# A hybrid attention layer on one Trainium2 core: where the low-rank stage takes its pages, which engine splits the weights, and how long the program's order waits behind tables and rows

## The chip, the cores and the metric

One core of a Trainium2 chip runs the whole layer. The metric is device time in microseconds of one execution. "Before" and "after" are two kernels that compute the same; the profile is one execution recorded by the hardware profiler. The engines are TensorE (PE, its weight loads PEld), VectorE (DVE), ScalarE (ACT), GpSimd (POOL) and SyncE (SP, which here only issues DMAs, in order).

## The reference

2048 tokens of width 1024 pass one layer. `h = rms_norm(x)`, one projection `h @ w_in`, and three groups of heads share its columns:

```python
c_q, c_kv, k_rope, gdn_qkv, gdn_a, gdn_b, mem_q, gate = split_cols(h @ w_in[l], IN_SPLITS)
q  = (rms_norm(c_q, q_a_norm[l]) @ w_q_b[l])       # low rank 384, then 4 heads, rotary part
kv = (rms_norm(c_kv, kv_a_norm[l]) @ w_kv_b[l])    # low rank 256
o_mla = causal_mla(...)
o_gdn = rms_norm(gated_delta_rule_chunked(...), gdn_norm[l])   # per chunk: T = (I + L)^-1, then a scan
o_mem = memory_attention(...)
x = x + (concat([o_mla, o_gdn, o_mem]) * silu(gate)) @ w_out[l]
return rms_norm(x, norm_final)
```

## The kernel before

All products that need fp32 accuracy are made of three passes: both operands are split into a high part (rounded to the fast format fp32r) and a low part (the rest), and `mm3` adds hi x hi, hi x lo and lo x hi. For the weights the split is `w_split` (L613): `copy` makes `wh` on ScalarE or VectorE, `lesser` (L628) chooses GpSimd or VectorE for `wl = w - wh`. A weight tile `wr` has two buffers, so the load of the tile after next, issued by SyncE, waits until `wl` has read its buffer.

The tokens are worked in two halves of 1024. In each half, 34 column tiles of `w_in` are streamed through TensorE (`ip`), and generators that were spawned by earlier tiles put their work between the products:

- `delta_head` (L843), four per half: norms (`sq`), decay rows (`gr`, loaded back from DRAM) and row factors (`fr`), the products `kk`, then a triangular solve of 31 steps on GpSimd (`pr`, `X`, fed and emptied by GpSimd's own DMAs), the block inverse (`inv`, `mid`), and a scan over 8 chunks. A chunk is a chain: `pa<-k,state` (TensorE), `r` (VectorE), `pa<-r,inv`, `vn` (ScalarE), `pa<-vn,kt`, the new state (VectorE), and beside it two products for the output. Only one scan runs at a time.
- `low_rank` (L1119), two per half ("the key rank" with 2 tiles, products `kb`, `vb`; "the query rank" with 3 tiles, `qb`): for each of two blocks of 512 tokens it loads the raw projection `craw`, squares and sums it, turns it (`sq`), makes the inverse root, spreads it (`rb`) and splits the scaled tiles (`chl`); then it streams small weights (`bw`) through `mm3`. It needs 2n pages of a pool of 10, of which each delta head also holds two or three. The last query tiles get their rotary part from tables (`cs`, `sn`) loaded by `trig_load` (L1183).

Behind the projections come causal attention (`sc`, `pt`, `av`), memory attention and the output projection (`op`).

Nothing of this order is decided on the chip. While the program is built, a planner runs beside it: `note`, `pool_cost`, `pool_dma` and `issue` keep a planned time for each engine, each generator is resumed when TensorE's planned time reaches the time that it yielded (`yield 2000` means 2 us behind the step's planned end), and the instructions are written in that order. Each engine then works its own list strictly in order, so the plan's numbers set which instruction stands in front of which.

Of the kernel before, what the change touches and what calls it, by code (L numbers as in the profile page):

```python
# [15 lines left out]
ALU = mybir.AluOpType  # L16
# [9 lines left out]
NH = 4  # L26
# [16 lines left out]
SPARE = 700.0  # L43
# [7 lines left out]
SLACK = {"wl": 500.0, "bwl": 0.0}  # L51
# [16 lines left out]
def hybrid_layer(ctx, tc, a, out):  # L68
    nc = tc.nc
    V, A, G, PE = nc.vector, nc.scalar, nc.gpsimd, nc.tensor  # L70
# [76 lines left out]
    T = {"PE": 0.0, "DVE": 0.0, "ACT": 0.0, "POOL": 0.0, "SP": 0.0, "DMA": 0.0}  # L147
# [5 lines left out]
    in_psum = set()  # L153
    tiles = set()
    step_end = [0.0]
    solving = [0.0]
    tab = [None]

    def free(ap):
        return int(np.prod(ap.shape[1:]))  # L160
# [61 lines left out]

    def pool_cost(op, args, kw, out):
        if op == "tensor_tensor":
            return 147 + 2.1 * free(out)
        fast = op == "tensor_scalar" and kw["op0"] == ALU.mult and kw.get("op1") == ALU.add
        return 160 + (0.85 if fast or op == "memset" else 3.4) * free(out)

# [18 lines left out]
    class Timed:  # L247
# [3 lines left out]
        def __getattr__(self, op):  # L251
            f = getattr(self.eng, op)

            def call(*args, **kw):
# [6 lines left out]

    V, A, G, PE = (Timed(nc.vector, "DVE", dve_cost), Timed(nc.scalar, "ACT", act_cost),
                   Timed(nc.gpsimd, "POOL", pool_cost), Timed(nc.tensor, "PE", pe_cost))


# [18 lines left out]
    def pool_dma(out, in_):  # L284

        touch(in_, out)
        t = max(T["POOL"], T["PE"], arrival(in_, "POOL"), used.get(out.tensor.name, 0.0),
                floor.get(out.tensor.name, 0.0)) + 600
        T["POOL"] = t
        t += 1500 + free(out) * out.shape[0] * 4 / 200  # L290
        wrote(out, "SP", t + 1000)
        step_end[0] = max(step_end[0], t + 1000)
        used[in_.tensor.name] = max(used.get(in_.tensor.name, 0.0), t + 200)
        pinned(nc.gpsimd.dma_start(out=raw(out), in_=raw(in_)))  # L294
# [32 lines left out]
    POLL = 800.0  # L327
# [22 lines left out]
    done = {}  # L350
# [9 lines left out]
    def take(**need):  # L360
        while not can(**need):
            yield POLL
        grab(**need)
# [250 lines left out]
    def w_split(w):  # L614
        wh = sb.tile([P, 512], F32R, name="wh", tag="wh", bufs=3)
        copy(wh, w)
        wl = sb.tile([P, 512], F32R, name="wl", tag="wl", bufs=3)
        lesser("wl").tensor_tensor(wl, w, wh, op=ALU.subtract)
        return wh, wl

    def copy(out, in_):
# [5 lines left out]

    def lesser(name):  # L628

        return G if max(T["POOL"], solving[0]) <= T["PE"] + SLACK[name] else V  # L630

    class Job:

# [207 lines left out]
        return consume  # L841

    def delta_head(hf, h, q, k, res):  # L843

        yield from take(N=1)
        sums, norms = (sb.tile([P, 16], F32, name=n, tag=n, bufs=b) for n, b in (("sums", 1), ("norms", 4)))
# [49 lines left out]
        for b in range(2):  # L896
            bs = slice(b * 512, (b + 1) * 512)
            nq, nb, ne = (t.rearrange("p (c t) -> p c t", t=P) for t in cur)

            gc = cols[:, 0, h * 8 + b * 4:h * 8 + b * 4 + 4]  # L900
            gr3 = gr.rearrange("p (c t) -> p c t", t=P)
            V.tensor_tensor(gr3, gr3, gc.unsqueeze(2).broadcast_to([P, 4, P]), op=ALU.subtract)
            V.tensor_tensor(gr3, gr3, neg.unsqueeze(1).broadcast_to([P, 4, P]), op=ALU.add)
            A.activation(gr, gr, AF.Exp)
            k3, q3 = (t[:, bs].rearrange("p (c t) -> p c t", t=P) for t in (k, q))
            V.tensor_tensor(kq[:, :, 0, :], k3, nb, op=ALU.mult)
            yield 0
            V.tensor_tensor(kq[:, :, 1, :], q3, nq, op=ALU.mult)
            V.tensor_tensor(q3, q3, ne, op=ALU.mult)
            V.tensor_tensor(gr3, gr3, nk[:, b * 4:b * 4 + 4].unsqueeze(2).broadcast_to([P, 4, P]), op=ALU.mult)  # L910
            yield 0
            if b == 0:
                cur = rows(1)
                yield SPARE
            for c2 in range(2):
                ps = psg("kk")
                for c in range(2):
                    cc = c2 * 2 + c
                    PE.matmul(ps[:, c * 256:(c + 1) * 256], k[:, b * 512 + cc * P:b * 512 + (cc + 1) * P],
                              kq[:, cc, :, :], start=True, stop=True)  # L920
                o = b * 4 + c2 * 2
                ps4 = ps.rearrange("p (c i t) -> p c i t", c=2, i=2)
                dec = gr3[:, c2 * 2:c2 * 2 + 2, :]
                V.tensor_tensor(LT[:, o:o + 2, :], ps4[:, :, 0, :], dec, op=ALU.mult)
                atm = sb.tile([P, 2, P], F32, name="atm", tag="atm", bufs=2)
                V.tensor_tensor(atm, ps4[:, :, 1, :], dec, op=ALU.mult)
                dma(out=at_d[hf][h][:, o * P:(o + 2) * P], in_=atm.rearrange("p c t -> p (c t)"), awaited=False)
                if b == 0 and c2 == 1:
                    gr = decay_row(1)
                yield 0  # L930
        give(A=1)
        done["rows"] = done.get("rows", 0) + 1
        for bk in range(4):
# [8 lines left out]
        pool_dma(out=X, in_=a["eye4"])  # L942
        for cs in range(4):
            pool_dma(out=lt[cs * 32:(cs + 1) * 32].rearrange("p j i -> p (j i)"), in_=lsys[hf][h])
        solving[0] = T["POOL"] + 25000
        yield 2000
        pr = sb.tile([P, 80], F32, name="pr", tag="pr", bufs=1)
        for j in range(31):
            n = j // 4 + 1
            w = 31 - j  # L950
# [3 lines left out]
            G.tensor_tensor(X[:, 0:n, j + 1:32], X[:, 0:n, j + 1:32], prv, op=ALU.subtract)  # L954
        for cs in range(4):
            pool_dma(out=tsys[hf][h].rearrange("s (n e) i -> e s n i", e=4)[cs], in_=X[cs * 32:(cs + 1) * 32])
        solving[0] = T["POOL"] + 12000
        yield from take(TT=1)
        yield 0
        give(lt=1)  # L960
# [8 lines left out]
        for n in (32, 64):  # L969
            pairs = [(2 * n * p, slice(2 * n * p, 2 * n * p + n), slice(2 * n * p + n, 2 * n * p + 2 * n))  # L970
                     for p in range(64 // n)]
            mid = t2("mid", (P, 8 * n))
            mid3 = mid.rearrange("p (c t) -> p c t", t=n)

            def sl(c):
                return slice(c * n, (c + 1) * n)
            for o, lo, hi in pairs:
                for i in range(n // 32):
                    for j in range(i, n // 32):
                        src, dst = slice(o + i * 32, o + i * 32 + 32), slice(o + j * 32, o + j * 32 + 32)  # L980
                        V.transpose(mid3[dst, :, i * 32:i * 32 + 32], TT[src, :, dst])
                        if i < j:
                            G.memset(mid3[src, :, j * 32:j * 32 + 32], 0.0)
            yield 0
            ps = psg("inv")
            for c in range(NCK):
                for o, lo, hi in pairs:
                    PE.matmul(ps[hi, sl(c)], LT[lo, c, hi], mid[lo, sl(c)], start=True, stop=True)
            for o, lo, hi in pairs:
                if o:  # L990
                    A.activation(mid[hi, :], ps[hi, 0:8 * n], AF.Copy, scale=-1.0)
                else:
                    V.tensor_scalar(mid[hi, :], ps[hi, 0:8 * n], -1.0, None, op0=ALU.mult)
            yield 0
            ps = psg("inv")
            for c in range(NCK):
                for o, lo, hi in pairs:
                    PE.matmul(ps[lo, sl(c)], mid[hi, sl(c)], TT[hi, c, hi], start=True, stop=True)
            for o, lo, hi in pairs:
                (A.copy if o else V.tensor_copy)(TT[lo, :, hi], ps[lo, 0:8 * n].rearrange("p (c t) -> p c t", t=n))  # L1000
            yield 0
# [15 lines left out]
        for c in range(NCK):  # L1017
# [32 lines left out]
            t = step_end[0]  # L1050
# [40 lines left out]
    def small_weights(srcs):  # L1091

        def load(src):
            w = sb.tile([P, src.shape[1]], F32, name="bw", tag="m2", bufs=9)
            dma(out=w, in_=src, awaited=False)
            return w

        def split(w):
            n = w.shape[1]
            wh = sb.tile([P, n], F32R, name="bwh", tag="m2", bufs=9)  # L1100
            copy(wh, w)
            wl = sb.tile([P, n], F32R, name="bwl", tag="m2", bufs=9)
            lesser("bwl").tensor_tensor(wl, w, wh, op=ALU.subtract)
            return wh, wl
        w = load(srcs[0])
        yield 2800
        cur = split(w)
        w = load(srcs[1])
        yield 0
        for i in range(len(srcs)):  # L1110
            nxt = None
            if i + 1 < len(srcs):
                nxt = split(w)
                if i + 2 < len(srcs):
                    w = load(srcs[i + 2])
            yield cur
            cur = nxt

    def low_rank(hf, n, gain, srcs, use):  # L1119

        yield from take(page=2 * n)
        hs, ls = ([[], []] for _ in range(2))
        for b in range(2):
# [20 lines left out]
        t = 0  # L1144
# [12 lines left out]
    def q_use():  # L1157
# [9 lines left out]
        def use(hf, t, hs, ls, wh, wl):  # L1167
# [10 lines left out]
            for b in range(2):  # L1178
# [1 line left out]
                cs, sn = t2("cs"), t2("sn")  # L1180
                trig_load(cs, 0, hf * 2 + b, 4)
                trig_load(sn, 1, hf * 2 + b, 4)
                yield 2000  # L1183
                r1, r2 = project(b, hs, ls, *half), project(b, hs, ls, wh, wl)
                tA, tB, tC = t2("ra"), t2("rb"), t2("rc")
                V.tensor_tensor(tA, r1, cs, op=ALU.mult)
# [1010 lines left out]
```

## Time and profile before

| | us |
|---|---|
| median of 3 runs | 1818.56 (1814.57 to 1819.68) |
| the profiled execution's own time | 1822.34 |
| its span, first to last instruction | 1820.6 |
| TensorE busy | 1746.9 (96%) |
| VectorE busy | 1158.6 (64%) |
| ScalarE busy | 734.6 (40%) |
| GpSimd busy | 500.4 (27%) |
| mean granted clock of TensorE | 0.983 |

A matmul counts as busy until its modelled end, and matmuls overlap; what TensorE loses shows as idle time before an instruction and as stretches with a granted clock below 1.0 (at 0.5 it runs at 1.2 instead of 2.4 GHz). An engine that is not TensorE matters where TensorE waits for it, or where it holds a DMA that someone else needs.

### The profile page before, as it was taken

How to read it: one execution, taken by the hardware profiler on the slowest of the kernel's cores; microseconds unless marked ns; L12 is line 12 of the kernel's file. 1: busy time of each engine (PE TensorE's matmuls, PEld its weight loads, DVE VectorE, ACT ScalarE, POOL GpSimd, SP SyncE). 2: the span in 40 equal slices, each digit the busy share in tenths (PEclk: the TensorE clock that was granted, in tenths of full speed). 3: DMA queues.
4: the chain of work that ended last, by engine and by line, in shares of the span. 5: the costliest groups of instructions: out<-in, count | busy, mean ns of one | idle time of the engine just before them, and what ended most of it. 6: DMA issues, size and time to landing. Idle time of an engine off the chain costs nothing.

```text
span 1820.6 us, 28632 instructions
## 1 busy us (share of the span) xinstructions
PE 1746.9 (96%) x9776; PEld 1471.2 (81%) x9776; DVE 1158.6 (64%) x2622; ACT 734.6 (40%) x1884; POOL 500.4 (27%) x894
## 2 busy tenths in 40 slices
PE   7999999999999999899999997999999999999998
PEld 5778788888777777788888876899999998888886
DVE  6777766786785858445566653777676778345443
ACT  6444233342442535213453423455455556222121
POOL 1422752443521124352112625001111012412120
PEclk9999999999999999999999998999999999999999
DMA  7544474456555344564555479145252527566551
GB/s 265 163 128 150 137 237 137 131 160 211 154 170 176 121 147 116 184 194 138 182 199 176 141 216 265 61 127 178 70 177 71 159 88 224 167 195 199 168 162 53
DMA packets 225826, 291.19 MB, mean 160 GB/s; under 512 B 30320, under 2 KB 130672, under 8 KB 225680
## 3 DMA queue, kind: packets, MB, share of 16 engines
q1 hardware_dynamic: 218640, 273.62, 48.3%
q0 software_dynamic: 7040, 15.74, 3.0%
q8 instruction: 77, 1.26, 0.3%
q14 instruction: 69, 0.57, 0.1%
HBM read 197.79 MB, written 91.49 MB: 159 GB/s over the span
## 4 chain that ended last, share of the span: by engine, by line
PE 54%; DMA 4%; DVE 3%; POOL 1%; issue 1%; ACT 1%; SPq 1%; DVEq 0%; ACTq 0%; POOLq 0%
PE op L259 14%; PE ip L259 13%; PE sc L259 9%; PE av L259 7%; PE pt L259 4%; PE pa L259 2%; PE qb L259 1%; PE inv L259 1%; DVE y L259 1%; PE kk L259 1%; DMA craw<-craw 1%; SPq L305 1%; PE kb L259 1%; PE mk L259 1%; POOL X L259 1%
## 5 line engine op out<-in xcount | busy, mean ns | idle before, releaser
L259 PE MATMUL ip<-hh,wh 128*128 128x512 f32 x1088 | 459.8, 423 | 12.6 <-ACT hh L259 9.1
L259 PE MATMUL ip<-hh,wl 128*128 128x512 f32 x1088 | 433.8, 399 | 5.1 <-DVE wl L259 4.0
L259 PE MATMUL ip<-hl,wh 128*128 128x512 f32 x1088 | 432.3, 397 | 0.0
L259 POOL TENSOR_TENSOR wl<-wr,wh 128x512 fp32r<-128x512 f32 x84 | 120.2, 1431 | 493.9 <-ACT wh L259 403.9
L259 PEld LDWEIGHTS ip<-hh,wl 128*128 128x128 f32 x1088 | 208.3, 191 | 52.7 <-DVE wl L259 4.5
L259 PEld LDWEIGHTS ip<-hh,wh 128*128 128x128 f32 x1088 | 209.1, 192 | 49.5 <-ACT hh L259 9.1
L259 PEld LDWEIGHTS ip<-hl,wh 128*128 128x128 f32 x1088 | 209.2, 192 | 35.4 <-DVE hl L259 0.5
L259 ACT CAST wh<-wr 128x512 fp32r<-128x512 f32 x144 | 88.9, 618 | 148.6 <-PE ip L259 99.1
L259 DVE TENSOR_TENSOR tl<-pt,th 128x512 fp32r<-128x512 f32 (+2 forms) x208 | 119.8, 585 | 32.6 <-ACT th L259 30.2
L259 PE MATMUL av<-th,vn 128*128 128x256 f32 x576 | 133.2, 290 | 1.9 <-ACT th L259 1.9
L259 PE MATMUL sc<-kn,qn 128*128 128x512 f32 (+2 forms) x480 | 134.0, 379 | 0.0
L259 PE MATMUL op<-wop,mh 128*128 128x512 f32 x416 | 130.6, 394 | 0.0
L259 DVE SCALAR_TENSOR_TENSOR y<-raw,gdn_conv,y 128x512 f32<-128x512 f32 x144 | 116.5, 814 | 16.1 <-ACT y L259 14.7
L259 ACT CAST th<-pt 128x512 fp32r<-128x512 f32 (+2 forms) x160 | 80.6, 512 | 105.6 <-PE pt L259 98.7
L259 POOL TENSOR_TENSOR pr<-X,lt 128x60 f32<-128x60 f32 (+24 forms) x248 | 92.4, 373 | 49.2 <-DMA lt<-lsys 30.3
L259 PEld LDWEIGHTS av<-th,vn 128*128 128x128 f32 x576 | 99.2, 189 | 6.8 <-ACT th L259 3.0
L259 POOL TENSOR_TENSOR X<-X,pr 128x60 f32<-128x60 f32 (+24 forms) x248 | 95.9, 386 | 19.4
L294 POOL DMA_DIRECT2D mix<-mo x64 | 34.8, 544 | 226.5 <-ACT mo L259 186.8
L259 PE MATMUL sc<-kr,qr 128*128 128x512 f32 (+2 forms) x320 | 96.7, 380 | 0.0
L259 ACT ACTIVATE s<-s,m 128x768 f32<-128x768 f32 (+13 forms) x71 | 79.0, 1114 | 41.7 <-DVE mx L259 35.2
L259 PEld LDWEIGHTS op<-wop,mh 128*128 128x128 f32 x416 | 77.4, 188 | 17.5
L259 PE MATMUL pt<-ident,s 128*128 128x128 f32 x544 | 84.2, 276 | 6.2 <-DVE vt L259 6.0
(285 smaller groups left out, 3522.5 us busy)
## 6 DMA issues: line engine op xcount, KB each, us to landing
wr<-in_w_in SPq DMA_DIRECT2D x148, 256.0 KB
fr<-rows_n SPq DMA_DIRECT2D x48, 256.0 KB
mxo<-mix SPq DMA_DIRECT2D x16, 768.0 KB
craw<-craw SPq DMA_DIRECT2D x40, 256.0 KB
x<-in_xT SPq DMA_DIRECT2D x32, 256.0 KB
gatem<-gt SPq DMA_DIRECT2D x32, 256.0 KB
qn<-qn SPq DMA_DIRECT2D x32, 256.0 KB
vn<-v SPq DMA_DIRECT2D x32, 256.0 KB
```

The costliest lines, as they stand in the source:

```text
L259: return pinned(f(*args, **kw))
L294: pinned(nc.gpsimd.dma_start(out=raw(out), in_=raw(in_)))
L305: ins = pinned(nc.sync.dma_start(out=raw(out), in_=raw(in_)))
```

## The change

- In the second half (`hf` = 1) `low_rank` asks for pages only when the fourth delta head has started (`done[("head", hf, h)]`, set by `delta_head` at its start).
- `w_split` and the small weights make their low part on VectorE always. `lesser` stays for the opening tiles alone; the guard `solving`, which kept splits off GpSimd during a planned solve, is gone.
- The plan's costs of GpSimd's elementwise work and of its DMAs are larger.
- The generators yield longer at four places: 2500 behind the issue of the second decay row, SPARE (700) twice per level of the inverse, 5000 instead of 2000 behind the rotary tables.

```diff
-    solving = [0.0]
...
         if op == "tensor_tensor":
-            return 147 + 2.1 * free(out)
+            return 290 + 2.25 * free(out)
...
-        t += 1500 + free(out) * out.shape[0] * 4 / 200
+        t += 2500 + free(out) * out.shape[0] * 4 / 200
...
         wl = sb.tile([P, 512], F32R, name="wl", tag="wl", bufs=3)
-        lesser("wl").tensor_tensor(wl, w, wh, op=ALU.subtract)
+        V.tensor_tensor(wl, w, wh, op=ALU.subtract)
...
-        return G if max(T["POOL"], solving[0]) <= T["PE"] + SLACK[name] else V
+        return G if T["POOL"] <= T["PE"] + SLACK[name] else V
...
     def delta_head(hf, h, q, k, res):
 
+        done[("head", hf, h)] = True
...
                 if b == 0 and c2 == 1:
                     gr = decay_row(1)
-                yield 0
+                    yield 2500
+                else:
+                    yield 0
...
-        solving[0] = T["POOL"] + 25000
...
-        solving[0] = T["POOL"] + 12000
...
-            yield 0
+            yield SPARE
             ps = psg("inv")
...
-            yield 0
+            yield SPARE
             ps = psg("inv")
...
-            lesser("bwl").tensor_tensor(wl, w, wh, op=ALU.subtract)
+            V.tensor_tensor(wl, w, wh, op=ALU.subtract)
...
     def low_rank(hf, n, gain, srcs, use):
 
+        while hf and not done.get(("head", hf, NH - 1)):
+            yield POLL
         yield from take(page=2 * n)
...
                 trig_load(sn, 1, hf * 2 + b, 4)
-                yield 2000
+                yield 5000
```

The plan's numbers move instructions on every engine: 95 splits from GpSimd to VectorE, and the order of most rows from the first weight product on. Three places show it.

GpSimd, second half, between the solves of the first and second head (`X`, `lt`, `pr` belong to the solve, `tsys` and `inv` carry its result to DRAM and back, `wl` is a weight split that reads the load buffer `wr`). Before:

```order
L259 TENSOR_TENSOR X_7109<-X_7109,pr_7223 128x8
L294 DMA tsys1_0_109<-X_7109 256x1x32 x4
L294 DMA inv0_279<-tsys1_0_109 32x8x32 x4
L294 DMA X_7847<-in_eye4 128x256
L259 TENSOR_TENSOR wl_7655<-wr_7553,wh_7653 128x512
L259 MEMSET mid_7770 32x8x32
L294 DMA lt_7846<-lsys1_1_102 32x1024 x4
L259 TENSOR_TENSOR pr_7934<-X_7847,lt_7846 128x31
```

In the change:

```order
L258 TENSOR_TENSOR X_7584<-X_7584,pr_7689 128x8
L293 DMA tsys1_0_109<-X_7584 256x1x32 x4
L293 DMA inv0_279<-tsys1_0_109 32x8x32 x4
L293 DMA X_8522<-in_eye4 128x256
L258 MEMSET mid_8365 32x8x32
L293 DMA lt_8521<-lsys1_1_102 32x1024 x4
L258 TENSOR_TENSOR pr_8635<-X_8522,lt_8521 128x31
```

The split of `wr_7553` stood behind eight DMAs of the solve; in the change GpSimd's list there holds the solve alone.

SyncE, second half, around the load of the second decay row `gr` (`at` stores a product of the same head, `bw` and `wr` are weight loads, `qn` stores of the query rank, `mk` stores and loads of the memory projection). Before:

```order
L305 DMA bw_7779<-in_w_q_b 128x384
L305 DMA at1_1_78<-atm_7575 128x256
L305 DMA wr_7857<-in_w_in 128x512
L305 DMA qn1_2_143<-ehi_7597 128x512
L305 DMA gr_7608<-rows_g_62 128x512
L305 DMA qn1_2_143<-elo_7598 128x512
L305 DMA at1_1_78<-atm_7606 128x256
```

In the change:

```order
L304 DMA wr_8374<-in_w_in 128x512
L304 DMA mk_197<-ehi_8112 128x256
L304 DMA mk_197<-elo_8113 128x256
L304 DMA bw_8180<-in_w_mk 128x512
L304 DMA gr_8168<-rows_g_62 128x512
L304 DMA at1_1_78<-atm_8127 128x256
L304 DMA bw_8230<-in_w_mv 128x512
L304 DMA at1_1_78<-atm_8166 128x256
```

The weight load `wr` stands two places ahead of `gr` before and four in the change; the query rank's stores have left this place, the memory projection's have come.

TensorE, second half, inside the scan of the fourth head (`pa`: steps of a chunk, `av`, `pt`: attention, `rb`: the spread of the query rank). Before:

```order
L259 MATMUL pa_12230<-st_odd_257,y_10185 128x128
L259 MATMUL av_12137<-th_12216,vn_11293 128x256
L259 MATMUL av_12137<-tl_12217,vn_11293 128x256
L259 MATMUL av_12137<-th_12216,vn_11294 128x256
L259 MATMUL av_12137<-th_12216,vn_11293 128x256
L259 MATMUL pt_12247<-ident_227,me_12066 128x128
L259 MATMUL pa_12230<-r_12232,inv1_280 128x128
L259 MATMUL av_12137<-tl_12217,vn_11293 128x256
L259 MATMUL av_12137<-th_12216,vn_11294 128x256
L259 MATMUL pt_12247<-ident_227,me_12066 128x128 x3
L259 MATMUL pa_12230<-vn_12242,kt_12102 128x128
```

In the change:

```order
L258 MATMUL pa_11171<-vn_11175,aT_10660 128x128
L258 MATMUL pa_11251<-st3_256,y_9159 128x128
L258 MATMUL pa_11251<-vn_11264,aT_11198 128x128
L258 MATMUL pa_11280<-st_odd_257,y_9543 128x128
L258 MATMUL pa_11280<-r_11282,inv1_280 128x128
L258 MATMUL pa_11280<-vn_11290,kt_11208 128x128
L258 MATMUL rb_11255<-dg_11243,ones_232 128x512
L258 MATMUL rb_11255<-dg_11245,ones_232 128x512
L258 MATMUL pa_11280<-st_odd_257,y_9159 128x128
L258 MATMUL pa_11280<-vn_11290,aT_11198 128x128
L258 MATMUL pa_11298<-st3_256,y_9543 128x128
```

Before, attention stands between the steps of a chunk; in the change the steps of the third and fourth head's scans stand next to each other here, and the query rank, which was done in the projections, is only at its spread.

## Rows read from the trace of the kernel before

**Rows 1.** the page, busy us (share of the span) and instructions of each engine
```profile
PE 1746.9 (96%) x9776; PEld 1471.2 (81%) x9776; DVE 1158.6 (64%) x2622; ACT 734.6 (40%) x1884; POOL 500.4 (27%) x894
```

**Rows 2.** table by stretches: us, engines' busy us (instructions), TensorE clock, DMA share, GB/s
```profile
76.00:1090.00 1014.00, 978.83 (x5320) 808.67 (x5319) 669.14 (x1336) 394.46 (x1082) 354.75 (x629) 0.99 0.52 163
1090.00:1175.00 85.00, 72.88 (x477) 61.72 (x476) 44.64 (x146) 29.43 (x91) 28.68 (x87) 0.88 0.63 178
```

**Rows 3.** the same table, six short windows
```profile
60.00:80.00 20.00, 17.21 (x63) 12.87 (x62) 13.88 (x43) 7.68 (x19) 10.23 (x11) 0.83 0.69 168
130.00:145.00 15.00, 10.97 (x42) 8.61 (x41) 14.94 (x22) 5.90 (x12) 6.61 (x3) 0.89 0.34 100
495.00:520.00 25.00, 22.19 (x140) 17.44 (x139) 20.14 (x43) 8.91 (x19) 4.39 (x4) 0.86 0.53 171
560.00:605.00 45.00, 39.11 (x182) 31.71 (x181) 29.01 (x46) 16.09 (x44) 5.28 (x4) 0.96 0.40 124
675.00:700.00 25.00, 19.55 (x81) 15.40 (x80) 18.11 (x39) 8.46 (x16) 4.35 (x3) 0.93 0.33 113
750.00:775.00 25.00, 19.62 (x132) 15.61 (x131) 10.94 (x22) 4.64 (x10) 4.02 (x7) 0.86 0.49 163
```

**Rows 4.** timeline of TensorE at three holes: start us, us, instruction [idle before <-releaser]
```profile
567.15 0.80 PE L259 MATMUL pa<-st,y 128*128 128x128 f32 x2 [2.39 <-DVE st_odd L259]
567.74 0.63 PE L259 MATMUL pa<-vn,aT 128*128 128x128 f32 x2
...
762.12 1.07 PE L259 MATMUL inv<-mid,LT 32*32 32x32 f32 x20 [5.28 <-DVE mid L259]
...
1130.84 0.87 PE L259 MATMUL pt<-ident,s 128*128 128x128 f32 x3 [6.04 <-DVE vt L259]
```

**Rows 5.** timeline of VectorE ahead of the same holes
```profile
562.55 0.69 DVE L259 TENSOR_TENSOR ra<-qb,cs 128x512 f32<-128x512 f32 x1 [6.57 <-DMA cs<-trig]
...
759.62 0.69 DVE L259 TENSOR_TENSOR gr<-gr,cols 128x512 f32<-128x512 f32 x1 [8.60 <-DMA aT<-at]
...
1127.18 0.69 DVE L259 TENSOR_SCALAR_CACHE_REDUCE s<-sc 128x512 f32<-128x512 f32 x1 [5.99 <-POOL pr L259]
```

**Rows 6.** timeline of SyncE's DMA queue, 745 to 755 us
```profile
745.43 0.97 SPq L305 DMA_DIRECT2D at<-atm  x1
753.76 0.33 SPq L305 DMA_DIRECT2D wr<-in_w_in  x1
...
754.67 0.38 SPq L305 DMA_DIRECT2D gr<-rows_g  x1
```

**Rows 7.** what SyncE's queue waited for, 100 to 1090 us: total, times, longest
```profile
SPq L305 <- POOL wl L259: 174.2, 54, 11.7
...
SPq L305 <- DVE wl L259: 75.8, 30, 8.5
```

**Rows 8.** the page's groups: GpSimd's weight split xcount | busy us, mean ns
```profile
L259 POOL TENSOR_TENSOR wl<-wr,wh 128x512 fp32r<-128x512 f32 x84 | 120.2, 1431 | 493.9 <-ACT wh L259 403.9
```

**Rows 9.** the same groups of VectorE, 0 to 1175 us
```profile
L259 DVE SCALAR_TENSOR_TENSOR y<-raw,gdn_conv,y 128x512 f32<-128x512 f32 x144 | 116.5, 814 | 16.1 <-ACT y L259 14.7
L259 DVE TENSOR_TENSOR wl<-wr,wh 128x512 fp32r<-128x512 f32 x64 | 45.9, 718 | 17.2 <-ACT wh L259 16.6 <-DMA wr<-in_w_in 0.2
L259 DVE SCALAR_TENSOR_TENSOR y<-raw,y 128x512 f32<-128x512 f32 x48 | 34.4, 719 | 9.1 <-ACT raw L259 8.6
```

**Rows 10.** groups of ScalarE: its table loads
```profile
L259 ACT ACT_TABLE_LOAD x4 | 5.1, 1283 | 0.8 <-PEq L2180 0.7
```

**Rows 11.** timeline of SyncE's queue, the query rank's loads of two blocks
```profile
670.34 1.38 SPq L305 DMA_DIRECT2D craw<-craw  x3
...
701.62 1.34 SPq L305 DMA_DIRECT2D craw<-craw  x3
```

**Rows 12.** timeline of VectorE, the second block's last splits
```profile
723.13 1.27 DVE L259 TENSOR_TENSOR chl<-craw,chl 128x512 fp32r<-128x512 f32 x2
```

## The prediction

> **What bounds the kernel now.** The first view is the page's busy table: TensorE works 1746.9 of 1820.6 us, VectorE 64%, GpSimd 27% [rows 1]. TensorE is the engine to fill; the change touches none of its arithmetic (the program has 9,010 TensorE instructions before and after), so time can only go where TensorE stands still or runs at half clock. Next the table by stretches: between 76 and 1090 us, the projections with the delta rule woven in, TensorE lacks 1014 - 978.8 = 35.2 us and its granted clock of 0.99 costs about another 10; in the 85 us before attention is dense it lacks 12.1 and the clock of 0.88 costs 10.2, together 22.3 [rows 2]. The same table by short windows shows six holes. Idle plus (1 - clock) x width gives 6.2 us at 60:80, 5.7 at 130:145, 6.3 at 495:520, 7.7 at 560:605, 7.2 at 675:700 and 8.9 at 750:775, 42.0 in all [rows 3]. Last the timelines, for what makes such a hole.
>
> At 762.1 TensorE waited 5.28 us for VectorE's `mid` [rows 4]. VectorE had stood 8.60 us before `gr<-gr,cols`, put down to a DMA [rows 5]. The DMA was late because SyncE's queue, which issues in order, stood from 746.4 (745.43 + 0.97) to 753.76 before a weight load `wr`, and the load of `gr` was two places behind it [rows 6]. The weight load waited for its buffer, whose last reader is a weight split on GpSimd; that split stands behind the DMAs of the triangular solve on GpSimd's queue, as the order rows show. It is no single case: from 100 to 1090 us SyncE waited 54 times, 174.2 us, for GpSimd's `wl` [rows 7]. The hole at 567 is of another kind: VectorE took the rotary product 6.57 us before its table had landed, and the scan step behind it came late [rows 4, 5]. The one at 1130.8 is a third: VectorE wanted a page that the solve on GpSimd still read, waited 5.99 us, and TensorE lost 6.04 [rows 4, 5].
>
> **The change part by part.**
>
> *Weight splits.* 84 `wl` and 11 `bwl` leave GpSimd (1431 ns each for the first kind [rows 8]) and go to VectorE at 718 ns [rows 9]: 95 x 0.718 = 68 us more, less a few for narrow tiles. Something comes back: GpSimd and VectorE slow each other. The convolution step has a mean of 814 ns, its sister on tiles of the same size 719 [rows 9]; over 144 of them that is 13.7 us, so VectorE's net is about +54 us in the first 1175. The Trainium skill ("SBUF — State Buffer", "Who interferes with whom") says that a VectorE instruction with two SBUF inputs and a GpSimd one that reads SBUF block each other whole. By that rule each of the 84 splits could hold VectorE for its 1.43 us, 120 us in all, and the move would unload VectorE; the rows bear out the direction and a ninth of the size, and the rows decide.
>
> The 54 us lie on an engine that was busy 669.1 of 1014 [rows 2] and goes from 66% to 71%. Bounds: nothing if TensorE's 11 us of matmuls per split cover it, 54 if nothing does. I take 6, since splits are made one load ahead: what is left of the 45 us of idle and clock in that stretch, some 22 us, grown by a quarter, as busy/(1 - busy) grows from 1.9 to 2.4.
>
> In return SyncE's queue no longer waits for GpSimd. The holes at 750:775 (8.9) and 675:700 (7.2) I count as gone; the second also loses the rank stage that stood in it.
>
> *Time behind tables and rows, and the solve's costs.* 5000 for 2000 behind the rotary tables, 2500 for 0 behind the second decay row, larger costs for GpSimd's work and DMAs, and SPARE in the inverse add no instruction. They let VectorE's in-order queue meet the consumer later. The table's hole is 2.39 + 1.8 of clock = 4.2 us of 560:605, gone. The other 3.5 there have other causes and stay. The holes at 60:80, 130:145 and 495:520, 18.2 us, lie where nearly every row has moved; VectorE is behind them too, and I count half, 9.1. Middle: 8.9 + 7.2 + 4.2 + 9.1 = 29.4 back, 6 spent: -23.4. ScalarE gets two more table loads of 1283 ns [rows 10]; it is busy 394 of 1014 [rows 2], so I cost them at nothing, and at 2.6 us if that cover fails. A scan started later costs nothing while projections fill TensorE.
>
> *The low-rank stage.* In the second half the `kb`, `vb` and `qb` products no longer fill the projections: the order puts all of them behind the last weight product or beside the very last ones. The delta rule's heads take their pages first, the query rank starts when the key rank returns its own, and that chain is now bare. SyncE's queue issues the query rank's loads right behind the stores of the last `vb`; from there two blocks follow each other. Before, one block took from 701.62 to 724.4, 22.8 us [rows 11, 12], the other, in a crowd, from 670.34 to 701.62, 31.3 [rows 11]. So the first `qb` can come 45.6 to 62.6 us after the last `vb`. Between the two stand 161 TensorE instructions, most of them scan steps of the third and fourth heads and the fourth head's inverse, often with nothing between one step and the next. 49 scan products are 98 records in a trace, at full clock about 0.15 each (two took 0.59 at half clock [rows 4]), 14.5 us; 64 others at the 0.153 of the tail (72.88 us over 477 [rows 2]) 9.8; the inverse's 48 small ones some 1.3 [rows 4]. That is 25.6 us, 32 if all 210 records cost 0.153. TensorE is idle 20 us there (13.6 to 37). Idle stretches come with half clock: the tail before lost 10.2 to it, and I take 10 again (5 to 15). The tail then costs 30 instead of 22.3: +8 (-4 to +30). The hole at 1130.8 is part of the 22.3 that goes.
>
> **Sum.** 1822.3 (the profiled execution; 1820.6 is its span) - 23.4 + 8 = 1806.9. It ran 3.8 above the median of 1818.6, so 1803 on the scale of the runs. Bounds for this case: middle gain 13 to 33, tail as taken: 1793 to 1815.
>
> **Rivals.**
>
> *The bare chain costs more than the middle returns.* Place: from the last `vb` to the first `qb`. For it: VectorE and SyncE serve scan, splits and rank at once there, and the slower of the two blocks was the one in a crowd. Against it: VectorE was busy only 44.6 of 85 in the old tail [rows 2]. At 62.6 us the tail takes 37 idle and 15 clock, +30, and with -20 in the middle the run gets to 1832 - 3.8 = 1828. It decides from where the two blocks take 61 us (61 - 25.6 + 10 - 22.3 = 23, the middle's gain).
>
> *VectorE becomes the limit, or SyncE waits on.* For it: it was busy 14.94 of 15 at 130:145 [rows 3], and a weight load still waits for its split, now on VectorE: 30 such waits cost 75.8 us, 2.5 each against 3.2 for GpSimd's [rows 7]. Then only a part of the middle's gain is left, about 8 us, and the tail takes it: 1818.5, no change. The skill's page "Perfetto Trace Analysis" ("Optimizing Scalar/DVE Operations") advises to take work off a saturated VectorE, to GpSimd even: the change does the reverse, and in that one window the trace agrees that VectorE is full; over the whole stretch, at 66%, it does not. Against the rival: splits on VectorE meet no solve in their queue.
>
> *Everything opens.* All 42.0 come back and the tail costs no more than before: 1822.3 - 42 - 3.8 = 1776.
>
> **How the numbers follow.** Forecast 0.45, bare chain 0.22, VectorE or SyncE 0.20, everything 0.13. About 0.3%, 5.5 us, is what a measurement tells from no change here, so "same" is 1813 to 1824. Faster: 0.43 of the forecast (its upper edge lies over 1813), 0.13, and 0.02 of the third case: 0.58. Same: 0.02 and 0.16: 0.18. Slower: 0.22 and 0.02 of a third case with a full VectorE: 0.24. The forecast's own range is 1793 to 1815. For 8 in 10 the range leaves out the better half of "everything" and the worst of the bare chain: 1781 to 1832.
>
> **What would show it.** Right: no `wl` among GpSimd's instructions and among what SyncE waits for; no wait over 5 us on VectorE for `gr` or `cs`; TensorE idle under 20 us from 76 us to the last projection; a hole of 15 to 25 us, in pieces of 0.3 to 2 us between scan steps at half clock, between the last `vb` and the first `qb`; attention from there on as dense as before. Wrong: waits of TensorE for VectorE's `wl` (VectorE is the limit), SyncE's waits for `wl` on VectorE as long as GpSimd's were, or 35 us and more between `vb` and `qb`.

## The result and the profile after

The change is slower by 1.5%: 1846.82 us in the median (1841.13 to 1851.35, 4 runs) against 1819.12 (1814.57 to 1826.69, 4 runs), a ratio of 1.015 with a 95% interval of 1.0119 to 1.0181. The profiled execution took 1847.79 us, its span is 1846.0, 25.4 longer than the one before.

The page after, busy us of each engine (answers to [rows 1]):

```profile
PE 1753.9 (95%) x9776; PEld 1477.1 (80%) x9776; DVE 1178.2 (64%) x2713; ACT 741.2 (40%) x1890; POOL 364.0 (20%) x799
```

GpSimd lost 136 us of work and VectorE gained 20, so the splits moved as written. To find where TensorE stands, three stretches of the changed kernel (columns as in [rows 2]):

```profile
76.00:500.00 424.00, 405.87 (x2164) 333.96 (x2163) 288.85 (x575) 158.03 (x432) 119.98 (x292) 0.98 0.48 149
500.00:1040.00 540.00, 521.00 (x2883) 430.06 (x2882) 342.33 (x718) 211.46 (x582) 101.45 (x245) 0.99 0.49 153
1040.00:1215.00 175.00, 144.48 (x841) 122.42 (x840) 110.19 (x307) 65.30 (x188) 29.54 (x86) 0.86 0.69 216
```

Width minus busy is idle time, and (1 - clock) x width is what half clock costs, but for the part of it that lies inside idle time. The table below gives the loss of every run, summed from the trace: idle time before TensorE's instructions, plus half of the time at half clock outside it. The losses are those of the profiled execution, which lies up to 5.2 us from the median (e3's that much under it). (The expectations count half clock inside idle time too; they say 26.6 and 54 where the table has 23.9 and 50.5.) The stretches are fixed in time, while the work in them moves: the last product of the projections ends at 1110.9 us before, at 1038.7 in the changed kernel, and between 1020.7 (e12) and 1123.1 (e1) in the others, so that what one stretch gains another can have got.

| kernel | median us | ratio to before | 76:500 | 500:1040 | 1040:1215 |
|---|---|---|---|---|---|
| before | 1819 | 1 | 12.2 | 33.4 | 24.1 |
| changed | 1846.8 | 1.0150 | 23.9 | 23.8 | 50.5 |
| e1: changed, no page wait | 1832.2 | 1.0082 | 19.4 | 28.6 | 32.5 |
| e2: before + page wait | 1834.6 | 1.0090 | 15.2 | 23.1 | 32.8 |
| e3: before + splits | 1845.5 | 1.0144 | 20.0 | 26.3 | 43.0 |
| e4: before + plan's numbers | 1838.2 | 1.0110 | 17.4 | 31.9 | 36.8 |
| e5: changed, key's tables later | 1840.3 | 1.0120 | 18.4 | 28.5 | 38.6 |
| e6: e1, last inverse later | 1826.0 | 1.0044 | 19.9 | 27.7 | 20.8 |
| e7: e6, key's tables later | 1819.9 | 1.0007 | 19.2 | 26.5 | 18.0 |
| e8: changed, only the key rank waits | 1842.1 | 1.0126 | 22.0 | 25.3 | 42.4 |
| e9: e7, first decay row later | 1811.3 | 0.9951 | 10.2 | 25.4 | 15.9 |
| e10: e4, last inverse later | 1840.4 | 1.0105 | 23.7 | 29.0 | 35.9 |
| e11: e3, all three places later | 1806.2 | 0.9926 | 15.2 | 17.9 | 24.8 |
| e12: changed, key's tables and row later | 1832.6 | 1.0066 | 8.4 | 33.0 | 38.7 |

So the stretch 500:1040 did gain, 9.6 us. The one ahead of it lost 11.7 and the tail 26.4. With the opening (4.0 gained) and the rest up to TensorE's last instruction (0.1 lost) that is +24.6, near the 25.4 of the spans.

**The middle.** Short windows of the changed kernel; the six of [rows 3], and three new ones:

```profile
60.00:80.00 20.00, 16.73 (x70) 13.13 (x70) 15.15 (x35) 6.75 (x17) 11.03 (x11) 0.91 0.54 114
110.00:125.00 15.00, 6.84 (x21) 5.49 (x22) 9.74 (x27) 2.74 (x7) 0.00 (x0) 0.66 0.25 75
130.00:145.00 15.00, 12.91 (x57) 10.36 (x57) 12.36 (x21) 4.86 (x10) 0.00 (x0) 1.00 0.21 64
495.00:520.00 25.00, 23.41 (x143) 18.71 (x142) 19.93 (x43) 10.90 (x32) 10.19 (x25) 1.00 0.77 257
560.00:605.00 45.00, 42.58 (x205) 34.61 (x204) 24.72 (x54) 16.46 (x41) 0.00 (x0) 1.00 0.39 126
615.00:630.00 15.00, 10.94 (x39) 8.67 (x38) 10.95 (x27) 3.33 (x9) 0.00 (x0) 0.77 0.34 112
655.00:667.00 12.00, 7.66 (x32) 6.09 (x31) 2.08 (x4) 2.16 (x5) 0.00 (x0) 0.86 0.25 84
675.00:700.00 25.00, 25.00 (x121) 20.70 (x121) 15.03 (x32) 11.36 (x36) 0.00 (x0) 1.00 0.50 171
750.00:775.00 25.00, 25.00 (x115) 20.68 (x113) 17.08 (x40) 10.67 (x25) 0.00 (x0) 1.00 0.53 165
```

The holes at 675:700 and 750:775 are gone, and the one behind the query's tables at 567 with them. New ones stand at 118, 622 and 662 us. The largest, in the timelines of VectorE and TensorE (idle time and releaser in brackets):

```profile
110.20 1.37 DVE L258 TENSOR_TENSOR ra<-kr,cs 32x512 f32<-32x512 f32 x2 [7.67 <-DMA cs<-trig]
...
118.16 0.37 PE L258 MATMUL rn<-ident,fac 128*24 128x128 f32 x1 [9.57 <-DVE fac L258]
```

VectorE took the rotary product of the key 7.67 us before its table had landed; the norms' factors `fac` are behind it in VectorE's list, and TensorE, also in order, stood before their transpose; of the half clock that came with it, 4.8 us lie behind the hole, so it cost 9.57 + 2.4 = 12.0 us. SyncE had issued the table at 102.86, behind a weight load at 100.66 that had waited 5.6 us for a split on VectorE. The hole at 662 is another engine's turn:

```profile
660.55 0.62 ACT L258 CAST bwh<-bw 128x512 fp32r<-128x512 f32 x1 [10.94 <-DMA bw<-in_w_mk]
...
661.91 0.52 PE L258 MATMUL pa<-vn,kt 128*128 128x128 f32 x2 [4.34 <-ACT vn L258]
```

ScalarE stood 10.94 us before a small weight that SyncE had issued at 651.40. Its weight copies for VectorE's split and the `vn` of a scan were behind it. This grew in general: VectorE's splits, and below them what SyncE's queue waited for from 100 to 1038 us (total, times, longest):

```profile
L258 DVE TENSOR_TENSOR wl<-wr,wh 128x512 fp32r<-128x512 f32 x148 | 102.8, 696 | 70.4 <-ACT wh L258 68.5 <-PE tr L258 1.2 <-issue 0.2
...
SPq L304 <- DVE wl L258: 239.5, 85, 12.3
```

In [rows 7] the queue waited 174.2 us for GpSimd's splits and 75.8 for VectorE's, 250 together. The name changed, the wait did not. VectorE now waits 68.5 us for ScalarE's `wh` where it waited 16.6 [rows 9].

**The tail.** The last 160 us before dense attention, cut at the last `vb` (1082.41) and the first `qb` (1138.91):

```profile
1040.00:1082.00 42.00, 38.41 (x242) 33.82 (x241) 28.80 (x81) 18.76 (x57) 23.14 (x70) 0.96 0.86 281
1082.00:1139.00 57.00, 40.16 (x265) 32.87 (x264) 37.61 (x105) 19.25 (x61) 4.43 (x11) 0.74 0.44 146
1139.00:1200.00 61.00, 50.91 (x243) 42.10 (x242) 34.03 (x90) 19.84 (x55) 0.00 (x0) 0.89 0.74 230
```

They lose 5.3, 28.6 (16.8 idle, 11.7 clock) and 15.9 us. The middle one is the query rank's bare chain, 56.5 us long. In the timelines of SyncE, VectorE and TensorE:

```profile
1089.31 1.59 SPq L304 DMA_DIRECT2D craw<-craw  x3
1097.04 8.31 SPq L304 DMA_DIRECT2D craw<-craw  x3
...
1119.00 1.89 DVE L258 TENSOR_TENSOR chl<-craw,chl 128x512 fp32r<-128x512 f32 x3
1132.43 1.89 DVE L258 TENSOR_TENSOR chl<-craw,chl 128x512 fp32r<-128x512 f32 x3
...
1121.20 0.80 PE L258 MATMUL pa<-r,inv 128*128 128x128 f32 x2 [3.94 <-DVE r L258]
1135.23 0.80 PE L258 MATMUL pa<-r,inv 128*128 128x128 f32 x2 [4.21 <-DVE r L258]
```

A block's scaling and splitting (three `craw`, three `chl`) stands in VectorE's list in front of a scan step's `r`, so the rank stage also holds the scan that should have covered it. The third piece is the end of the same stage:

```profile
1168.01 0.69 DVE L258 TENSOR_TENSOR ra<-qb,cs 128x512 f32<-128x512 f32 x1 [6.83 <-DMA cs<-trig]
...
1172.33 1.01 PE L258 MATMUL sc<-kn,qn 128*128 128x256 f32 x3 [3.54 <-DVE rc L258]
1180.64 1.31 PE L258 MATMUL sc<-kn,qn 128*128 128x512 f32 x3 [2.26 <-DVE rc L258]
...
1197.32 0.73 PE L258 MATMUL sc<-kr,qr 128*128 128x512 f32 x2 [3.59 <-DMA qr<-qr]
```

The last query tile's tables land late, its rotary products follow on VectorE, and the scores stand behind them, at 1197 behind the reload of the finished rotary part (`qr`).

### The profile page after: what moved, and what is told of

The parts are those of the page before. It is cut to its first block, busy times and chain, and to the rows that moved or that the text cites. A ratio compares the mean times of both kernels' runs of the same rounds, so it can differ in the third digit from the quotient of the medians.

```text
span 1846.0 us, 28583 instructions
## 1 busy us (share of the span) xinstructions
PE 1753.9 (95%) x9776; PEld 1477.1 (80%) x9776; DVE 1178.2 (64%) x2713; ACT 741.2 (40%) x1890; POOL 364.0 (20%) x799
## 5 line engine op out<-in xcount | busy, mean ns | idle before, releaser
L258 PE MATMUL ip<-hh,wh 128*128 128x512 f32 x1088 | 454.8, 418 | 10.3 <-ACT hh L258 8.0
L258 DVE TENSOR_TENSOR wl<-wr,wh 128x512 fp32r<-128x512 f32 x148 | 102.8, 696 | 70.4 <-ACT wh L258 68.5
L293 POOL DMA_DIRECT2D lt<-lsys x32 | 16.0, 504 | 573.6 <-DMA lsys<-LT 573.6
L258 DVE SCALAR_TENSOR_TENSOR y<-raw,gdn_conv,y 128x512 f32<-128x512 f32 x144 | 106.7, 749 | 17.5 <-ACT y L258 16.5
L258 POOL TENSOR_TENSOR X<-X,pr 128x60 f32<-128x60 f32 (+24 forms) x248 | 91.9, 371 | 19.4
L258 PEld LDWEIGHTS sc<-kn,qn 128*128 128x128 f32 x480 | 81.6, 193 | 15.2 <-DVE rc L258 6.5
```

The source lines that it names most:

```text
L258: return pinned(f(*args, **kw))
```

## Experiments

Each kernel is timed beside the kernel before on the same chip.

**e1, the changed kernel without the page wait.**

```diff
-        while hf and not done.get(("head", hf, NH - 1)):
-            yield POLL
         yield from take(page=2 * n)
```

> The changed kernel without its wait for pages in the second half; all else stays. Theory (the bare rank chain is the loss): between 1040 and 1200 us the changed kernel lost 30.5 us of idle time and 23 us of half clock, against 22.3 and little more before; with the rank work back among the projections that falls to 20 to 30, so the time is 1815 to 1822 us, and no wait of over 3 us stands between scan steps behind the last projection. Rival (the splits on VectorE are the loss, and the chain only shows it): the tail stays above 40 us and the time above 1835. If the hole of 9.57 us at 118 us stays, it is a matter of the other parts, as this edit does not touch the first half.

1832.17 us, ratio 1.0082 (1.0068 to 1.0096): 14.6 under the change, where some 27 were expected. The bare rank chain is gone, but another wait came out in the tail:

```profile
1139.37 0.43 DVE L258 STREAM_TRANSPOSE mid<-inv 32x256 f32<-32x256 f32 x1 [13.55 <-DMA inv<-tsys]
...
1142.69 0.58 PE L258 MATMUL av<-th,vn 128*128 128x256 f32 x1 [15.26 <-DVE th L258]
```

VectorE stands for the result of the fourth head's triangular solve, and attention's softmax is queued behind. With the page wait that solve came 46 us earlier (the loads of its result begin at 1086.6 us against 1133.1), and VectorE waited for it only 3.2 us. So the page wait does buy something, and pays more for it. The hole at 118 stayed (8.12 us).

**e2, the kernel before with the page wait alone.** The lines of e1 added, and `done[("head", hf, h)] = True` at a head's start.

> The kernel before with the wait for pages alone. Theory (bare chain): 1838 to 1855 us, with 45 to 60 us between the last product of the rank that goes first and the first product of the other, and the loss in the last 100 us before dense attention. Rival (the chain costs only together with the splits on VectorE): under 1828.

1834.61 us, ratio 1.0090 (1.0077 to 1.0103), a little under the range. Here the query rank went first, and between its last product (1104.7) and the key rank's first at 1120.8 only some 16 us passed, not 45 to 60; the tail lost 32.8, and attention behind 1215 us another 11.6, against 3.4 before. The page wait is a loss without the splits too.

**e3, the kernel before with the splits on VectorE.** `lesser(...)` becomes `V` in `w_split` and for the small weights, `solving` goes.

> The kernel before with only the weight splits on VectorE (and the guard for solves gone). Theory of the prediction: SyncE waits less, the holes at 675 to 700 and 750 to 775 us go, 1804 to 1814 us. Rival, as the changed kernel's trace has it (SyncE's queue waits for the splits as long as before, 240 us against 248, now on VectorE, and VectorE now stands 68 us before the splits for ScalarE's high parts instead of 14): 1815 to 1825, no gain. Third: 1828 and more, if the splits make VectorE late for the scans.

1845.52 us, ratio 1.0144 (1.0129 to 1.016): the third case. The hole at 118 is here (9.81 us), and the tail's hole is of e1's kind, with the last solve 21 us later than before (its loads begin at 1119.6 us against 1098.2):

```profile
1160.76 0.76 DVE L258 STREAM_TRANSPOSE mid<-inv 32x256 f32<-32x256 f32 x2 [11.86 <-DMA inv<-tsys]
...
1161.34 0.28 PE L258 MATMUL inv<-mid,LT 32*32 32x32 f32 x2 [11.57 <-DVE mid L258]
```

**e4, the kernel before with the plan's numbers alone** (the yields of the change and GpSimd's costs).

> The kernel before with only the plan's numbers changed: the longer yields at rows, inverse and tables, and GpSimd's larger costs. Theory of the prediction: a part of the 13 us at the tables and in the first half comes back, 1808 to 1817 us, and VectorE's wait of 6.57 us for the rotary table at 562 is under 3. Rival: the order moves holes elsewhere, 1817 to 1825.

1838.17 us, ratio 1.0110 (1.0095 to 1.0125): worse than either case. VectorE's wait at 562 is gone as expected, but the last solve began some 20 us later than before (its loads at 1117.7 us), VectorE stood 9.94 us for it, TensorE 10.79, and the fourth head's scan ran bare at half clock behind it.

The next three put one consumer or both later in the plan; e8 lets one rank go ahead.

**e5, the changed kernel, key's tables later.** `key_rope`: `yield 7000` for `yield 2000` behind the table loads.

> The changed kernel with 7000 instead of 2000 behind the key's rotary tables, nothing else. Theory (VectorE takes the key's rotary product 7.67 us before its table has landed, as SyncE's queue stood before a weight load; TensorE's hole of 9.57 us at 118 and 10.2 us of half clock follow from it): the hole goes, 76 to 500 us lose 10 to 14 us instead of 26.6, and the time falls by 10 to 16, to 1831 to 1837 us. Rival (VectorE is late there for its splits, the table is only the last wait by chance): another wait of over 5 us stands in its place, 1843 to 1850.

1840.33 us, ratio 1.0120 (1.0101 to 1.014), between the two. As the rival has it, another wait stands in the place, though not one for splits:

```profile
113.75 0.69 DVE L258 TENSOR_TENSOR gr<-gr,cols 128x512 f32<-128x512 f32 x1 [7.69 <-DMA gr<-rows_g]
...
116.94 0.37 PE L258 MATMUL rn<-ident,fac 128*24 128x128 f32 x1 [9.02 <-DVE fac L258]
```

The first decay row, issued behind the tables at 104.55, was now the first to be wanted and late. By the table the first stretch gained 5.5 us all the same, the second lost 4.7, and the tail gained 11.9.

**e6, e1 with the last inverse later.**

```diff
-        yield 4000
+        yield 16000 if hf and h == NH - 1 else 4000
```

> The changed kernel without the page wait, and the inverse of the second half's fourth head put 12 us later in the plan (16000 for 4000 behind its loads). Theory (VectorE stands in order before the solve's result for 13.55 us while attention's softmax is queued behind it, TensorE's hole of 15.26 us): the hole goes or falls under 4 us, and the run comes to 1815 to 1822 us instead of 1832. Rival (attention itself has nothing to do there before the head is through): the hole stays over 10 us under another name, 1828 to 1836.

1825.98 us, ratio 1.0044 (1.0027 to 1.0061), 6.2 under e1 and between the two cases. The hole of 15.26 became one of 5.69, at another place:

```profile
1132.96 0.58 PE L258 MATMUL av<-tl,vn 128*128 128x256 f32 x1 [5.69 <-POOL tl L258]
```

The tail's loss went from 32.5 to 20.8, and the two profiled executions, which the table is read from, lie 11.5 us apart as well (1835.15 and 1823.68); the medians moved by half of that, with e6's eleven runs spread from 1818.0 to 1830.3.

**e7, both** (e6 and e5's edit).

> Both edits, with no page wait: what the splits and the plan give when the two places where VectorE stands in order are gone. Theory: the two add up, 1800 to 1808 us, faster than the kernel before. Rival (splits on VectorE cost by themselves): 1816 and more, although no wait of over 5 us is left before VectorE's transposes and rotary products.

1819.85 us, ratio 1.0007 (0.9997 to 1.0017): as fast as before, and 12 us above the range. It is the rival's time without the rival's condition, as the hole at 117 (9.15 us) is left, with `gr` as in e5.

**e8, the changed kernel, only the key rank waits.** `while hf and n == 2 and ...`.

> The changed kernel with only the key rank waiting for the fourth head; the query rank takes its pages as before. Theory: the eighth solve is through before the projections end, as in the changed kernel, and one bare chain is left instead of two, with no rotary part at its end: 1040 to 1215 us lose 30 to 40 us instead of 54, 1825 to 1835 us. Rival (the query rank's pages hold the heads back, and the solve comes late): 1835 to 1845, with VectorE waiting for the last solve's result over 8 us.

1842.1 us, ratio 1.0126 (1.0108 to 1.0144), the rival: the last solve is late again, and the key rank's chain is bare besides. That the query rank's six pages hold the heads back fits, but was not shown apart.

```profile
1141.53 0.43 DVE L258 STREAM_TRANSPOSE mid<-inv 32x256 f32<-32x256 f32 x1 [12.13 <-DMA inv<-tsys]
...
1145.26 1.07 PE L258 MATMUL inv<-mid,LT 32*32 32x32 f32 x32 [13.30 <-DVE vt L258]
```

**e9, e7 with the first decay row later.** In `delta_head`, ahead of `gr, cur = decay_row(0), rows(0)`:

```diff
+        if not (hf or h):
+            yield 6000
```

> The run with the late inverse and the key's tables, no page wait, and now the first head's first decay row loaded 6 us later in the plan, so that VectorE's queue has the norms' factors ahead of the rotary product and of the decay row. Theory (TensorE's hole of 9 us at 117 us is VectorE standing in order before whichever load comes behind the key's tables, whose train runs at 50 GB/s for 8 us): the hole falls under 4 us, 76 to 500 us lose 8 to 13 us instead of 21.8, 1805 to 1812 us. Rival (VectorE is late there for its splits): a hole of over 6 us stays, 1816 to 1822.

1811.25 us, ratio 0.9951 (0.9934 to 0.9968), as the theory has it: no wait of TensorE over 0.4 us is left between 95 and 140 us. (One of 3.97 us for a split, at 143.2, stays; the kernel before has its like, 4.03 us at 137.4.) The row of this run's first stretch:

```profile
76.00:500.00 424.00, 415.27 (x2229) 340.01 (x2228) 298.64 (x596) 159.69 (x440) 122.66 (x305) 1.00 0.50 160
```

**e10, e4 with the last inverse later.**

> The kernel before with the plan's numbers (as in the run of the plan alone, 1838 us) and the fourth head's inverse 12 us later. Theory: VectorE's wait of 9.94 us for the last solve and TensorE's hole of 10.79 us go, and so does most of the half clock behind it, 1816 to 1826 us. Rival (the last solve is itself the end of the chain, 20 us later than before, and the scan behind it is bare): the hole goes, but the scan comes later still, 1832 to 1842.

1840.36 us, ratio 1.0105 (1.0083 to 1.0127): the rival's time, and less moved than either said. VectorE's transposes kept their places in its list and waited 10.13 us. The solve is what is late. Its queue on GpSimd shows a part:

```profile
1119.36 1.98 POOL L294 DMA_DIRECT2D lt<-lsys  x4
1129.99 0.57 POOL L294 DMA_DIRECT2D mix<-mo  x1 [8.45 <-ACT mo L259]
```

The solve had its input issued by 1121.34, but a store of attention stood in front of its first step and waited 8.45 us for ScalarE. The rest is older: the head's system (`LT`) was finished at 1113 us, against 1086 before. Which of the plan's numbers makes this head late was not tried.

**e11, e3 with the three places later** (the edits of e5, e6 and e9).

> The kernel before with the splits on VectorE (1845.5 us alone) and the three delays of the run above: the key's tables, the first decay row, the last inverse. Theory (the splits cost nothing by themselves, but move three waits to the front of VectorE's queue): 1812 to 1824 us. Rival (54 us more work on VectorE cost TensorE 15 us and more by themselves): 1832 and more.

1806.18 us, ratio 0.9926 (0.9905 to 0.9947), below the range, faster than both kernels and the fastest of the study: 39 us under e3. It is not a pure count of the three waits, because the plan also swapped the ranks (the key rank was through at 810 us, the query rank at 1124; in e3 at 929 and 790). And no run has the three delays without the splits, so it shows that the splits need not cost, not that they pay.

**e12, the changed kernel with the key's tables and the decay row later,** page wait kept.

> The changed kernel, with its page wait, and the delays behind the key's tables and before the first decay row. Theory (the page wait is a loss of its own, 15 to 20 us, in the bare rank chain): 15 to 20 us above the run without the wait, 1822 to 1832 us, with 40 to 57 us lost between 1020 and 1200 us. Rival (the page wait and the early solves pay once the hole at 117 us is gone): under 1815.

1832.58 us, ratio 1.0066 (1.0046 to 1.0087), just above the range: 21.3 above e9, which differs from it by the page wait and by the late inverse. Its first stretch is the best of all (8.4), its second loses 33.0 against e9's 25.4, and its tail 38.7 against 15.9, with the change's own waits back in it:

```profile
1101.86 0.80 PE L258 MATMUL pa<-r,inv 128*128 128x128 f32 x2 [4.16 <-DVE r L258]
1120.17 0.80 PE L258 MATMUL pa<-r,inv 128*128 128x128 f32 x2 [3.38 <-DVE r L258]
1158.56 1.01 PE L258 MATMUL sc<-kn,qn 128*128 128x256 f32 x3 [3.64 <-DVE rc L258]
```

## Why the prediction was wrong

It forecast 1803 us, faster, and the time lies 15 us above its range. Two of its terms failed. By the stretches of the trace either alone would have turned the sign: with the measured middle the sum is 1822.3 - 2.2 + 8 - 3.8 = 1824, with the measured tail 1822.3 - 23.4 + 30 - 3.8 = 1825. By the runs the middle is the larger: without the page wait (e1) the splits and the plan's numbers cost 14 us, tail included, where 23.4 were to come back.

**The tail, +8 forecast.** The bare chain itself: 45.6 to 62.6 us from the last `vb` to the first `qb`, measured 56.5; 20 us idle and 10 of clock, measured 16.8 and 11.7. That these fit is luck in part: the 20 belong to a chain of 45.6 with 25.6 us of TensorE's work in it, while the chain took 11 us more and TensorE was busy 40.2 of it. The step that failed is "The tail then costs 30 instead of 22.3", which let the tail begin at the last `vb` and end at the first `qb`. The stage goes on behind its products: tables, rotary products and the scores that need them cost 15.9 more, and the 42 us ahead of it 5.3. So the tail lost 49.7 where 30 stood. The old tail's 22.3 is 19.8 when half clock inside idle time is left out, as it is in the 49.7, so the tail lost 30 more and not 8. The pairs of runs confirm its sign and half to seven tenths of its size: the page wait costs 14.6 us (changed against e1), 16.6 (e2 against before) and 21.3 (e12 against e9, which has the late inverse besides). Against e1 it is less than 30 because there VectorE's wait for the last solve takes a part of the place (TensorE's hole of 15.26 us); why it is less in the other two was not traced.

**The middle, -23.4 forecast.** Measured: 49.9 us lost before in 76 to 1090 us, 47.7 after in 76 to 1040, where its projections end: 2.2. What was to come back did: counted as the prediction counts, the six windows of [rows 3] lost 42.0 before and some 11 after, 31 back where 29.4 stood. 675:700 and 750:775 went whole, 560:605 gave 5.3, and the three of which it took half gave 9.5 of their 18.2. The step that failed is the price set against this, "I take 6": close to 30 us of new losses stand in its place. It let the losses that were left grow by a quarter with VectorE's busy share, and so had no room for a hole that was not there before. (Two of its figures are off besides, by too little to matter: the stretch lost 50.4 us and not 45, as the 0.99 is a rounded clock that costs 15.2, and with 29.4 of the 45 back 16 are left, not 22.) The cost came by VectorE's order: the new list brought a load's consumer to its front before the load had landed, and the hole at 118 took 12.0 us; those at 622 and 662, behind late loads on VectorE and ScalarE, took 7.1 and 6.1 with their clock. The prediction's own sign, no wait over 5 us on VectorE for `cs`, failed twice: 7.67 us at 110.20 and 6.83 at 1168.01. That the splits by themselves need not cost this is shown by e9 and by e11: with the splits on VectorE and the late consumers moved, the first stretch loses 10.2 instead of the change's 23.9, and 15.2 instead of e3's 20.0 (12.2 before), and e11 is 39 us faster than e3. e11 comes to 1806 us, near the forecast, but without the page wait and the plan's numbers, and with three more edits.

**SyncE's queue.** "In return SyncE's queue no longer waits for GpSimd" is true by name alone. The prediction had noted 2.5 us per wait on VectorE against 3.2 on GpSimd, and had put this case among its rivals; it measured 239.5 / 85 = 2.8 each. That such waits need not be a loss is seen from e11 (72 of them, 208.4 us from 100 to 1038 us, and the best time); in the changed kernel one, of 5.6 us, stands ahead of the late table load at 102.86.

**VectorE's work.** +54 us forecast, +19.6 measured. The splits added 56.9 us by their own row (102.8 against 45.9 [rows 9]), so some 37 came back from VectorE's other work (some 3 of them four casts that ScalarE took over), not 13.7: the convolution step's mean fell from 814 ns [rows 9] to 749, the small operations gained too.

```profile
L258 DVE SCALAR_TENSOR_TENSOR y<-raw,gdn_conv,y 128x512 f32<-128x512 f32 x144 | 106.7, 749 | 17.5 <-ACT y L258 16.5
```

With the splits off GpSimd it is 748 to 750 in e1 and e3 as well; with 83 of the 95 still there (e4) it is 791. By the Trainium skill ("SBUF — State Buffer", "Who interferes with whom") a VectorE instruction with two SBUF inputs contends with a GpSimd one that reads SBUF, so a gain is what it expects; the trace has about a third of the 120 us that full blocking would give, where the prediction had seen a ninth. No time came of it: VectorE is busy 64% of the span before and after.

**The rivals.** None held as written. The nearest is the first, "The bare chain costs more than the middle returns", at 1828: its sign is right. But its deciding figure, two blocks of over 61 us, was not reached (56.5), and its place, from the last `vb` to the first `qb`, lost 28.6 us, about the 30 of the forecast; the run is slower because the middle returned nothing and the tail goes on behind the chain. Of the second, "SyncE waits on" came as written, 2.8 us per wait, but its time of 1818.5 needs a tail that takes 8 us.

**What stays open.** Why the plan's numbers alone (e4, e10) and the splits alone (e3) put the last solve some 20 us later, how much of e11's gain is the swapped ranks, and what the three delays would give the kernel before without the splits.

## What to carry to other kernels

When in-order engines share a program order, a moved instruction is priced by what it then stands in front of, more than by its length: for every engine that gets work or loses it, list the first instruction in each stretch that waits for a DMA or for another engine's long chain, and see who is queued behind it. A stage that is deferred must be followed to its very last consumer, through table loads, stores and reloads, before its bare length is summed. And where each part of a change loses when it is tried alone (e2, e3 and e4 all did), the kernel before may be matched to its plan; then try to move the few waits that came to the front, as e11 did, before the part is given up. One such move need not help (e10).

## What the runs showed of the hardware

In the changed kernel the loads of the key's rotary tables, 64 partitions wide, move slowly. From 85 to 120 us, 40 slices of 0.875 us, the DMAs' rate:

```profile
GB/s 227 119 0 0 73 227 0 330 243 45 0 0 166 133 0 0 0 0 0 241 286 293 232 133 159 26 51 51 49 51 51 47 51 47 28 0 47 253 150 88
```

From 107 to 115 us it is 50 GB/s, about a sixth of the 290 just before; the ten slices sum to some 395 KB, as much as the three table loads of 128 KB that were issued from 102.86 to 104.56. The width is not the reason: `kr<-krr`, 64 partitions and 128 KB too, was issued at 101.68, ahead of them, and has no part in these slices, which the tables fill. What sets the tables apart is that `trig_load` reads the same rows several times, in two copies for the key and in four for the query (256 KB each, four of them issued from 1161.2 to 1164.5). Six us of each, in the columns of [rows 2]:

```profile
108.00:114.00 6.00, 0.60 (x3) 0.17 (x1) 2.71 (x7) 0.00 (x0) 0.00 (x0) 0.89 0.13 50
1169.00:1175.00 6.00, 2.67 (x8) 2.28 (x9) 4.13 (x16) 0.62 (x2) 0.00 (x0) 0.65 0.26 98
```

With four copies the rate is 98 GB/s and the busy share of the DMA engines 0.26, twice the 50 and the 0.13 of two copies. So the late table ahead of the hole at 118 may have a second cure beside a later consumer, a load that repeats nothing. No run tried it, and why the rate goes with the copies is not shown.

In e5 the decay row that was issued behind these tables at 104.55 us was usable at 113.75, 9.2 us later.

TensorE's clock fell in or right behind each of the three longest holes of the middle (0.66, 0.77 and 0.86 in the rows 110:125, 615:630 and 655:667 above). Around the 9.57 us that end at 118.16 the granted clock is at its lower level, 1.2 instead of 2.4 GHz, from 112.7 to 122.9 us, so the work right behind a hole pays too, here 2.4 us more.
